# A column roll of an 8192 x 8192 matrix: all long row pieces issued on SP's ring, where SP and ACT had alternate rows

## The chip, the cores and the metric

The kernel runs on one core of one Trainium2 chip. The metric is the device time of one execution in microseconds (us), lower is better. Times before are given as the median of four runs; the profile is of one further execution. A core has 16 DMA engines; transfers reach them through rings (queues): one hardware ring for the transfers that SP issues, one for those of ACT, and a software ring for those of POOL.

## The reference

```python
def setup_inputs():
    return {
        "x": np.random.randn(8192, 8192).astype(np.float32),
        "shift": 100,
    }

def reference(x, shift):
    return np.roll(x, shift, axis=1)
```

Each row is rotated right by 100 columns: output columns 100 to 8191 are input columns 0 to 8091, and output columns 0 to 99 are the input's last 100. It is data movement alone: 268.4 MB in, 268.4 MB out.

## The kernel before

With `shift` 100, `s` is 100, and `a`, the column that divides the two ways of moving data, is 256 (100 rounded up to 128, plus 128, since it is at most 384). `g` is 156.

**Long row pieces** (line 43). Output columns 256 to 8191 are copied from HBM to HBM, without going through on-chip memory. Rows are taken in 128 blocks of 64 (`blocks`, loop variable `c`). In a block, the 64 rows are seen as 16 groups (`e`) of 4 consecutive rows (`j`). One DMA moves row `j` of all 16 groups: 16 rows of 7,936 floats (31,744 B each), 496 KB, one row for each DMA engine. The list `engines` (line 25) gives rows `j` = 0 and 2 to SP (`nc.sync`) and `j` = 1 and 3 to ACT (`nc.scalar`). In the last four blocks each DMA is cut in two column halves at `mid` (column 4224), 248 KB each. That makes 124 x 4 = 496 whole and 4 x 4 x 2 = 32 half DMAs: 248 whole and 16 half on each of the two engines.

**Heads** (lines 68 to 82). Output columns 0 to 255 go through on-chip memory on POOL's software ring. For each of 4 groups of 2,048 rows, POOL loads three tiles `t` of leading pieces (line 73) and two parts of `h` (lines 74 and 77), DVE copies pieces from `t` into `h` (lines 75 and 78), and after all loads POOL writes each `h` with four DMAs (line 82), 16 in all. That is 36 DMAs.

**What sets the order.** Each engine issues its DMAs in the order of the program. The tile framework gives every DMA from SP or ACT one of eight semaphores, DMAHW0 to DMAHW7, in turn, and a DMA waits until the earlier one with its semaphore has landed. As the two engines alternate, SP's DMAs have the semaphores 1, 3, 5, 7 and ACT's 0, 2, 4, 6: the first four on each engine wait for no transfer, and each later one waits for the one four places before it on its own engine, which is eight places before it in the program. There is no other wait between pieces, since they touch disjoint parts of the output. POOL's DMAs have semaphores of their own and wait for earlier loads, for DVE's copies and for their own earlier writes.

On a DMA engine, a row shows in the trace as one packet of 31,744 B (15,872 B for a half), followed on its ring by a packet of 4 B, which counts up the DMA's semaphore. Head packets have up to 4,400 B.

Of the kernel before, what the change touches and what calls it, by code (L numbers as in the profile page):

```python
# [1 line left out]

# [4 lines left out]


@with_exitstack
def kernel(  # L10
    ctx: ExitStack,
    tc: tile.TileContext,
    x: bass.AP,
    shift: int,
    out: bass.AP,
):
    nc = tc.nc
    n_rows, n_cols = x.shape
    s = shift % n_cols
    a = -(-s // 128) * 128  # L20
    if 0 < a <= 384 and a + 128 <= n_cols:
        a += 128
    g = a - s
    P = nc.NUM_PARTITIONS
    engines = [nc.sync, nc.scalar]
    n_chunks = 16
    rows = n_rows // n_chunks

    xm = x.rearrange("(c e j) w -> c j e w", e=16, j=4)
    om = out.rearrange("(c e j) w -> c j e w", e=16, j=4)
    if a < n_cols:
        blocks = n_rows // 64
        mid = (a + n_cols) // 256 * 128
        for c in range(blocks):
            parts = ((a, mid), (mid, n_cols)) if c >= blocks - 4 and a < mid else ((a, n_cols),)  # L40
            for j in range(4):
                for lo, hi in parts:
                    engines[j % 2].dma_start(out=om[c, j, :, lo:hi], in_=xm[c, j, :, lo - s:hi - s])
    if a == 0:
        return


    if a > 512:
        for i in range(n_chunks):
            r = slice(i * rows, (i + 1) * rows)  # L50
            nc.gpsimd.dma_start(out=out[r, :s], in_=x[r, n_cols - s:])
            if g > 0:
                nc.gpsimd.dma_start(out=out[r, s:a], in_=x[r, :g])
        return

    Q, J = 4, 4  # L60
    n_st = n_rows // (P * Q * J)
    reads = ctx.enter_context(tc.tile_pool(name="reads", bufs=n_st))
    heads = ctx.enter_context(tc.tile_pool(name="heads", bufs=n_st))
    xt = x.rearrange("(k p j q) c -> k q p j c", q=Q, j=J, p=P)
    ot = out.rearrange("(k p j q) c -> k q p j c", q=Q, j=J, p=P)
    tiles = []
    for k in range(n_st):
        t = reads.tile([P, Q - 1, J, a], x.dtype)
        h = heads.tile([P, Q, J, a], x.dtype)
        for q in range(1, Q):  # L70
            lead = bass.AP(tensor=x.tensor, offset=(k * P * J * Q + q) * n_cols - s,
                           ap=[[J * Q * n_cols, P], [Q * n_cols, J], [1, a]])
            nc.gpsimd.dma_start(out=t[:, q - 1], in_=lead)  # L73
        nc.gpsimd.dma_start(out=h[:, Q - 1, :, :s], in_=xt[k, Q - 1, :, :, n_cols - s:])  # L74
        nc.vector.tensor_copy(h[:, :Q - 1, :, :s], t[:, :, :, :s])  # L75
        if g > 0:
            nc.gpsimd.dma_start(out=h[:, 0, :, s:], in_=xt[k, 0, :, :, :g])  # L77
            nc.vector.tensor_copy(h[:, 1:, :, s:], t[:, :, :, s:])  # L78
        tiles.append(h)
    for k, h in enumerate(tiles):  # L80
        for q in range(Q):
            nc.gpsimd.dma_start(out=ot[k, q, :, :, :a], in_=h[:, q])  # L82


# [1 line left out]
_INS = ['x', 'shift']  # L86
_OUTS = [((8192, 8192), 'float32')]

_NUMBERS = {'shift': 100}


# [26 lines left out]
```

## Time and profile before

| what | value |
|---|---|
| median of 4 runs | 817.65 us (816.1 to 818.37) |
| the profiled execution's own time | 817.73 us |
| its span, first to last instruction | 815.6 us |
| DVE busy | 7.7 us, 8 instructions |
| POOL busy | 28.8 us, 40 instructions |
| bytes moved by the DMA engines | 276.89 MB, 340 GB/s over the span |
| DMA packets | 21,573, of them 9,025 under 512 B |

The span is read from the first to the last instruction of the core; the execution's own time has some 2 us more around it. Busy times of engines leave out the instructions that issue DMAs on SP and ACT. "Share" beside a DMA queue is the time its packets took, as a share of the span of 16 DMA engines; the share of a stretch is the mean busy share of these engines. GB/s counts each byte moved once, also where it is read from HBM and written to HBM. The time of a DMA "to landing" runs from its issue to the last count on its semaphore. The queues q1 and q10 are the two hardware rings of SP and ACT, and q0 is POOL's software ring.

### The profile page before, as it was taken

What the parts mean: (1) busy time and instruction counts of PE and PEld (TensorE: products, weight loads), DVE (VectorE), ACT (ScalarE), POOL (GpSimd) and SP (SyncE); (2) the same over time, 40 slices, a digit from 0 to 9 for tenths busy, and PEclk for the clock granted to TensorE, in tenths of its full rate; (3) what the DMA queues carried; (4) which work ended last, traced back from release to release, by engine and by line L of the source; (5) the groups of instructions that cost most, each with busy time, mean ns of one, the idle gap of its engine ahead of it and who ended that gap; (6) DMA issues with size and microseconds to landing.
All of it is one profiled execution on the core that took longest, in us unless ns stands there. A gap on an engine that the chain in (4) does not pass through costs nothing. (4 is left out here: it accounts for less than half of the span.)

```text
span 815.6 us, 633 instructions
## 1 busy us (share of the span) xinstructions
DVE 7.7 (1%) x8; POOL 28.8 (4%) x40
## 2 busy tenths in 40 slices
DVE  0000000000000000000000000000000000000000
POOL 3000000000010000000000000000000000000000
DMA  9999999999999999999999999999999999999998
GB/s 312 345 344 343 347 349 344 358 355 352 348 349 365 351 359 352 358 353 358 337 332 333 330 335 339 330 335 336 332 332 332 334 326 349 325 335 333 330 309 297
DMA packets 21573, 276.89 MB, mean 340 GB/s; under 512 B 9025, under 2 KB 9025, under 8 KB 13121
## 3 DMA queue, kind: packets, MB, share of 16 engines
q1 hardware_dynamic: 8448, 130.04, 46.5%
q10 hardware_dynamic: 8448, 130.04, 45.5%
q0 software_dynamic: 4672, 16.78, 7.0%
q14 instruction: 5, 0.03, 0.0%
HBM read 268.44 MB, written 268.44 MB: 658 GB/s over the span
## 5 line engine op out<-in xcount | busy, mean ns | idle before, releaser
L82 POOL DMA_DIRECT2D out_dram<-h x16 | 13.2, 825 | 196.2 <-DMA out_dram<-h 109.8
L73 POOL DMA_DIRECT2D t<-in_x_dram x12 | 9.5, 793 | 60.3 <-DMA h<-in_x_dram 30.2
L75 DVE COPY h<-t 128x1200 f32<-128x1200 f32 x4 | 3.1, 784 | 232.3 <-DMA t<-in_x_dram 232.3
L78 DVE COPY h<-t 128x1872 f32<-128x1872 f32 x4 | 4.9, 1224 | 0.0
L74 POOL DMA_DIRECT2D h<-in_x_dram x4 | 3.0, 747 | 45.7 <-DMA t<-in_x_dram 45.7
L77 POOL DMA_DIRECT2D h<-in_x_dram x4 | 3.0, 749 | 41.5 <-DMA t<-in_x_dram 41.5
L99 POOL MEMSET const-float32-0.0<- 128x1 f32 x1 | 0.1, 98 | 0.2 <-issue 0.2
L99 POOL MEMSET const-bfloat16-1.0<- 128x1 bf16 x1 | 0.1, 102 | 0.0
L99 POOL MEMSET const-float32-1.0<- 128x1 f32 x1 | 0.1, 99 | 0.0
L99 POOL MEMSET const-uint8-127<- 128x1 uint8 x1 | 0.1, 99 | 0.0
## 6 DMA issues: line engine op xcount, KB each, us to landing
out_dram<-in_x_dram SPq DMA_DIRECT2D x248, 496.0 KB, 12.6
out_dram<-in_x_dram ACTq DMA_DIRECT2D x248, 496.0 KB, 12.6
out_dram<-h POOLq DMA_DIRECT2D x16, 512.0 KB, 113.2
t<-in_x_dram POOLq DMA_DIRECT2D x12, 512.0 KB, 95.1
out_dram<-in_x_dram SPq DMA_DIRECT2D x16, 248.0 KB, 6.0
out_dram<-in_x_dram ACTq DMA_DIRECT2D x16, 248.0 KB, 6.1
h<-in_x_dram POOLq DMA_DIRECT2D x4, 312.0 KB, 93.4
h<-in_x_dram POOLq DMA_DIRECT2D x4, 200.0 KB, 97.4
```

What stands on the lines that cost most here:

```text
L73: nc.gpsimd.dma_start(out=t[:, q - 1], in_=lead)
L74: nc.gpsimd.dma_start(out=h[:, Q - 1, :, :s], in_=xt[k, Q - 1, :, :, n_cols - s:])
L75: nc.vector.tensor_copy(h[:, :Q - 1, :, :s], t[:, :, :, :s])
L77: nc.gpsimd.dma_start(out=h[:, 0, :, s:], in_=xt[k, 0, :, :, :g])
L78: nc.vector.tensor_copy(h[:, 1:, :, s:], t[:, :, :, s:])
L82: nc.gpsimd.dma_start(out=ot[k, q, :, :, :a], in_=h[:, q])
L99: nc = _bacc.Bacc("TRN2", target_bir_lowering=False, num_devices=1)
```

## The change

The list of two engines goes, and line 43 (42 in the changed kernel) issues every long piece from SP. Pieces, their sizes and their order stay; the heads stay on POOL.

```diff
-    engines = [nc.sync, nc.scalar]
     n_chunks = 16
     rows = n_rows // n_chunks
...
             for j in range(4):
                 for lo, hi in parts:
-                    engines[j % 2].dma_start(out=om[c, j, :, lo:hi], in_=xm[c, j, :, lo - s:hi - s])
+                    nc.sync.dma_start(out=om[c, j, :, lo:hi], in_=xm[c, j, :, lo - s:hi - s])
```

In the built program ACT has no DMA any more, and SP has 496 whole and 32 half ones in the order in which both engines had them. The eight semaphores go round over SP's DMAs alone: its first eight wait for no transfer, and each later one waits for the one eight places before it. POOL's and DVE's instructions are the same.

## The prediction

> **What bounds the kernel now.** I first read the table of stretches (columns: window, its length, busy us and instructions of DVE and of POOL, TensorE clock, mean busy share of the 16 DMA engines, GB/s moved) and the DMA queue rows of the page.
>
> ```profile
> 0.00:20.00 20.00, 0.00 (x0) 6.31 (x12) 1.00 0.91 310
> 20.00:200.00 180.00, 5.87 (x6) 12.37 (x15) 1.00 1.00 349
> 200.00:380.00 180.00, 1.83 (x2) 10.17 (x13) 1.00 1.00 354
> 420.00:600.00 180.00, 0.00 (x0) 0.00 (x0) 1.00 1.00 334
> 600.00:780.00 180.00, 0.00 (x0) 0.00 (x0) 1.00 0.99 333
> 780.00:800.00 20.00, 0.00 (x0) 0.00 (x0) 1.00 0.88 296
> 800.00:816.00 16.00, 0.00 (x0) 0.00 (x0) 1.00 0.79 291
> ```
>
> ```profile
> q1 hardware_dynamic: 8448, 130.04, 46.5%
> q10 hardware_dynamic: 8448, 130.04, 45.5%
> q0 software_dynamic: 4672, 16.78, 7.0%
> ...
> HBM read 268.44 MB, written 268.44 MB: 658 GB/s over the span
> ```
>
> The DMA engines are busy from start to end; no compute engine matters. The GB/s column seems to say that three rings (349, 354) are faster than two (334, 333). It counts each byte once, though, while a row piece touches HBM twice (read and write) and a head byte once (its other side is on chip). In 20 to 200 us the queue rows of that window give 55.34 MB of pieces and 7.45 MB of heads: (2 x 55.34 + 7.45) / 180 us = 656 GB/s at HBM. In 200 to 380 us: (2 x 55.85 + 7.79) / 180 = 664. In 420 to 780 us, with two rings: (2 x 119.79 + 0.28) / 360 = 666. So HBM traffic is level while the number of working rings falls from three to two.
>
> The packet records tell the same. I put them in order engine by engine (the trace names no engine, but a record begins within 4 ns of the end of the one before it on its engine, so nearly all chain up). A whole row, 31,744 B, takes 1.173 us at its fastest, 27.1 GB/s per engine or 433 GB/s for 16. Its mean is 1.37, 1.43 and 1.51 us in the three stretches: where head packets (159 ns each) take engine time, rows get shorter. Engines thus wait in their rows for something that they share, about 0.34 us of 1.51, and HBM is what fits.
>
> Next, the waits of the SP queue and the landing times of the issues:
>
> ```profile
> SPq L43 <- DMA out_dram<-in_x_dram: 670.1, 260, 4.0
> ```
>
> ```profile
> out_dram<-in_x_dram SPq DMA_DIRECT2D x248, 496.0 KB, 12.6
> out_dram<-in_x_dram ACTq DMA_DIRECT2D x248, 496.0 KB, 12.6
> out_dram<-h POOLq DMA_DIRECT2D x16, 512.0 KB, 113.2
> ```
>
> Of 264 issues on SP, 260 wait: each DMA has one of eight semaphores and waits for the DMA eight places before it. The program order has semaphores 1, 3, 5, 7 on SP and 0, 2, 4, 6 on ACT, so four DMAs are in flight on each. 12.6 us is about eight times the 1.55 us that one row DMA costs the machine (815.6 / 528).
>
> **The change, part by part.** Bytes, pieces, their order and the 36 POOL DMAs are unchanged. In the new program order SP has all 528 DMAs, with semaphores 0 to 7 in turn: each still waits for the one eight before. The total in flight stays eight, on one ring.
>
> Removed: 264 ACT issues of 516 ns (136 us), all beside transfers and off the path. Added on SP: 264 x 510 ns = 135 us. At the start SP's issues are 0.63 us apart (1.33, 1.98, 2.61 us from the first event), so SP needs 528 x 0.63 = 333 us of a span of 816; the cover is the eight DMAs in flight. Value: nothing. Without the cover a piece would wait 0.63 us for its issue; the bound would be 333 us, still far below.
>
> Start: a first issue lands rows on all 16 engines, each row needs at least 1.17 us, and the next issue comes 0.63 us later; one ring fills the engines. Nothing.
>
> Last four blocks: 32 half pieces of 248 KB, one per 0.72 us now (14 pairs of issues in 20.3 us). SP at 0.63 has little room, and a delay of one issue (0.5 us) is no longer covered by six microseconds of queue so well: up to +2 us. Against it, a piece's semaphore packet now follows its own data; today the order on an engine is mostly row of one ring, row of the other, then both semaphore packets, so that the first waits for a neighbour's row. Slots come free earlier: down to -2 us. I take 0, since the two act on the same wait.
>
> Heads: engines take turns between rings. Today a software packet comes once in about every row; with one hardware ring it gets a turn after the row and one after its semaphore packet, up to two per row. The heads can finish near 200 instead of 385 us, but nobody waits for them, and the HBM bytes are the same: nothing, if HBM sets the pace.
>
> The one price that the trace does not show in bulk is the order **row, semaphore, row, semaphore** on one ring. In the records there are 83 places where an engine did row, semaphore, row of one ring with nothing between: the gap ahead of the second row has a median of 4 ns, and a quarter of these rows take 1.175 us, the minimum. So there is no fixed bubble. But where an engine alternates row and semaphore for three rows or more (307 runs, any ring), it spends 1.540 us per row, 1.4% over the others at that moment; where it does two rows and then two semaphores (1,567 runs), 1.509, 1.4% under. Upper bound: 528 x 0.031 = 16 us, if nothing absorbs it. Lower bound: 0, or below by what earlier release gives (6 us, see the third case). An engine's cost is taken out of its 0.34 us of waiting for HBM, and stretches with 2 to 3% idle engines move no less at HBM (600 to 620 us: share 0.986, 671 GB/s). So I take 0 and keep both ends.
>
> The Trainium skill, "DMA: Bandwidth & Descriptors", section "Queues, rings and completion order", speaks against the change: a semaphore increment is a strongly ordered write, landing only after every earlier write of that engine. The same page, "Latency and other measured facts", gives HBM access as 0.2 us on average and 2 us under high load. If a ring stood still for 0.2 us per row, an estimate by that page, 528 of them would add 106 us; the 4 ns gaps above do not show that, though they are few.
>
> Sum: the profiled execution was 817.73 us (span 815.6 and 2.1 around it); 817.7 + 0 + 0 + 0 = **817.7 us**, against a median of 817.65.
>
> **The rivals.**
> - **Slower: the semaphore packet after every row costs engine time that HBM does not absorb.** For it: the 1.540 against 1.509 us. Against it: the level HBM rate and the 4 ns gaps. It applies all through, and decides once the cost exceeds what the engines now wait for HBM. Full price 817.7 + 16 = 834; with half absorbed, 826. I give 826.
> - **One ring holds fewer than eight DMAs.** The trace shows four on a ring, never more. With half the bytes in flight, the nearest row is the half-piece stretch at 296 GB/s against 333: 817.7 x 333 / 296 = 920. It is the case where the change does not do what the semaphores say.
> - **Faster: earlier release and shorter stalls.** Share 0.88 and 0.79 in the last 36 us is 20 x 0.12 + 16 x 0.21 = 5.8 us idle, of which 1.6 us lie after the last data; 0.5% idle in 420 to 780 us is 1.8 us. If all goes: 817.7 - 4.2 - 1.8 = 811.7. Half of it and a little from HBM, which no row prices: 812. That HBM itself moves more with rows going strictly in turn cannot be excluded: its 20 us stretches in 420 to 780 us lie between 648 and 683 GB/s, so 1% or so (8 us) below 812, 804, is the far end.
>
> **How the numbers follow.** A measurement of this kernel can tell about 0.2% (1.6 us) from no change. HBM cap, no change: 0.38. Slower at 826: 0.34. One ring too short: 0.02. Faster at 812: 0.26. A part of the first case falls just outside 1.6 us on either side, and a part of the outer ones inside, so faster is 0.28, same 0.34, slower 0.38. The range 804 to 834 us takes in both bounds of the semaphore cost and the faster case; outside it remain the short ring and larger movements of HBM. The forecast's own range is 816 to 819.5.
>
> **What would show it.** Right: SP's waits fall from 670 to about 500 us (816 less 333), landing stays near 12.5 us, one hardware queue at some 92% of the engines, HBM near 658 GB/s, heads done near 200 us. The slower case: the mean of a whole row still near 1.5 us or above after the heads, with the mean rate after 420 us under 330 GB/s and landing above 12.6. Short ring: SP's waits gone into long issues and engine share near 0.9. Faster: the last two rows of the table of stretches above 300 GB/s and the share there above 0.9. The forecast is wrong if the HBM rate with only one ring at work leaves 655 to 675 GB/s.

## The result and the profile after

The changed kernel takes 818.38 us (median of 52 runs, 816.18 to 822.52), the kernel before 816.93 us (median of 76 runs). The ratio is 1.0020, 95% interval 1.0014 to 1.0026: 1.6 us slower by the ratio, 1.5 us by the medians, just at the border of what the prediction called no change. The profiled execution took 819.14 us, with a span of 817.0. In the experiments, which all ran on one chip, the kernel before takes 830 us, so each of them is given with its ratio to the kernel before as it ran beside it.

The stretches, with the columns of the table before (window, length, busy us of DVE and of POOL, clock, share of the DMA engines, GB/s):

```profile
0.00:20.00 20.00, 0.00 (x0) 7.04 (x13) 1.00 0.91 321
20.00:200.00 180.00, 7.70 (x8) 21.80 (x27) 1.00 1.01 362
200.00:380.00 180.00, 0.00 (x0) 0.00 (x0) 1.00 1.00 341
420.00:600.00 180.00, 0.00 (x0) 0.00 (x0) 1.00 1.00 332
600.00:780.00 180.00, 0.00 (x0) 0.00 (x0) 1.00 1.00 332
780.00:800.00 20.00, 0.00 (x0) 0.00 (x0) 1.00 0.94 314
800.00:817.00 17.00, 0.00 (x0) 0.00 (x0) 1.00 0.86 300
```

The DMA engines are as full as before. POOL's work, which reached past 370 us, is now done in the second row: in 20 to 200 us GB/s rises from 349 to 362, since more of the bytes are head bytes that touch HBM once. At HBM nothing rose. The queue rows of that stretch (packets, MB, share) are

```profile
q1 hardware_dynamic: 3324, 52.77, 78.1%
q0 software_dynamic: 3467, 12.40, 22.8%
```

which makes (2 x 52.77 + 12.40) / 180 us = 655 GB/s, against 656 before. From the page, the queues over the whole span, and HBM:

```profile
q1 hardware_dynamic: 16896, 260.08, 92.7%
q0 software_dynamic: 4672, 16.78, 6.7%
...
HBM read 268.44 MB, written 268.44 MB: 657 GB/s over the span
```

One ring carries what two carried, 92.7% against 46.5 + 45.5%, and HBM moves 657 GB/s against 658. SP's waits and the issues, with KB each and us to landing:

```profile
SPq L42 <- DMA out_dram<-in_x_dram: 529.0, 499, 2.0
```

```profile
out_dram<-in_x_dram SPq DMA_DIRECT2D x496, 496.0 KB, 12.4
out_dram<-h POOLq DMA_DIRECT2D x16, 512.0 KB, 59.2
out_dram<-in_x_dram SPq DMA_DIRECT2D x32, 248.0 KB, 5.5
```

SP issues twice as often and still waits 529 us for landings; a whole DMA lands in 12.4 us, so eight are in flight. POOL's writes land in 59 us where they took 113: the software ring gets its turns more often. In 20 to 200 us it moved 12.40 MB, before 7.45. The last head DMA has landed at 262 us, before at 485.

Where do the 1.6 us lie? I summed the packet records' HBM bytes over time in both profiles. The two stay within about 1 us of each other until half of the bytes are through (270 of 537 MB: 412.8 and 413.8 us), then the changed kernel falls behind slowly, by 2.4 us at 510 MB, and ends 1.5 us behind. In the stretch without heads it moves 663 GB/s at HBM, before 667. In this pair of profiles it is a small loss along the second half, with no single wait in it. One pair of profiles cannot place so small a loss; a second pair, under the last experiment, does not repeat it there.

### The profile page after: what moved, and what is told of

Its sections match the earlier page's. It is cut to its first block, busy times and chain, and to the rows that moved or that the text cites. A ratio compares the mean times of both kernels' runs of the same rounds, so it can differ in the third digit from the quotient of the medians.

```text
span 817.0 us, 633 instructions
## 1 busy us (share of the span) xinstructions
DVE 7.7 (1%) x8; POOL 28.8 (4%) x40
## 2 busy tenths in 40 slices
DMA packets 21572, 276.89 MB, mean 339 GB/s; under 512 B 9024, under 2 KB 9024, under 8 KB 13120
## 3 DMA queue, kind: packets, MB, share of 16 engines
q1 hardware_dynamic: 16896, 260.08, 92.7%
## 6 DMA issues: line engine op xcount, KB each, us to landing
out_dram<-in_x_dram SPq DMA_DIRECT2D x496, 496.0 KB, 12.4
```

## The experiments

Four theories of the small loss were put to the test. Theory A: the semaphore packet right after each row costs the single ring some HBM rate. Theory B: the heads, which now finish early, cause it. Theory C: SP's issues limit. Theory E, formed after the first runs: one ring moves a little less in the long stretch and wins some back in the half pieces. The experiments ran in three sets, each with the kernel before beside it.

**Without heads, two rings and one.** The function returns after the long pieces:

```diff
-    if a == 0:
+    if a < n_cols:
         return
```

> This kernel leaves the heads out (output columns 0 to 255 are not written) and has the long pieces on SP and ACT as before. It is the partner of the next one. Both theories: 520.1 MB of HBM traffic at the 0.6665 MB per us that the kernel before showed between its last head packet and its first half piece is 780.4 us; with 2.7 us before the first data, about 0.7 us lost in the half pieces and 2.1 us around the span, about 786 us.

> Heads left out (output columns 0 to 255 are not written), all long pieces on SP. Theory A (a semaphore packet right after every row makes the single ring move less at HBM, 0.6635 against 0.6665 MB per us in the stretch without heads): the loss is there without heads too and longer, 520.1/0.6635 = 783.9 us, so about 3 us slower than the partner with two rings, less 1 us gained in the half pieces: +2 to +3 us. Theory B (the loss comes from the heads, which are done by 261 instead of 485 us and leave a longer stretch without them, or from their double turns): no heads, no loss: within 1 us of the partner, or faster by the 1 us gained at the end.

Measured: 800.06 us with two rings (ratio 0.9643, 0.9625 to 0.9661) and 800.32 us with one (0.9641, 0.9622 to 0.9659). With heads the kernel before took 830.5 us in this set. The 786 us expected for two rings was for a kernel before of 817 us; 0.9643 of that is 788. No loss of one ring can be seen here, which speaks against theory A and for B, as far as intervals of 0.2% on either side reach: the 2 to 3 us that A expected lie at their edge. The pair says something about the bound too. The pages' HBM rows:

```profile
HBM read 260.05 MB, written 260.05 MB: 652 GB/s over the span
```

(the same for both kernels). Without heads the bytes that DMA engines move fall by 6.1% (276.89 to 260.05 MB), those at HBM by 3.1%; the time falls by 3.6%. That is much nearer to the fall at HBM than to that at the engines; 0.5% is left over.

**Two rows per engine in a DMA.**

```diff
+    xi = x.rearrange("(c e j) w -> c e j w", e=16, j=4)
+    xo = out.rearrange("(c e j) w -> c e j w", e=16, j=4)
...
+            if c < blocks - 4:
+                for j in range(0, 4, 2):
+                    nc.sync.dma_start(out=xo[c, :, j:j + 2, a:n_cols], in_=xi[c, :, j:j + 2, a - s:n_cols - s])
+                continue
```

With two rings, `engines[j // 2]` stands in place of `nc.sync`.

> As before, but each whole DMA takes two consecutive rows per DMA engine (32 rows, 992 KB; rows 0 and 1 on SP, 2 and 3 on ACT), the last four blocks as they were. Half as many semaphore packets and twice the bytes in flight. Theory A: a semaphore packet costs engine time, which two rings already halve by taking them in pairs; at most 1 to 2 us faster than before. Theory B: no change within 1 us.

> Two rows per engine and DMA as in the kernel above, all on SP. The order on an engine is row, row, semaphore packet. Theory A: as many semaphore stops as in the two-ring kernel before, so the loss of one ring is gone or halved: 0 to 1 us against the two-ring partner, 1 to 2 us faster than the changed kernel. Theory B: the heads get their turns at a different rhythm still, the loss of 1.5 to 2 us against the two-ring partner stays.

Measured: 842.07 us (1.0134, 1.0110 to 1.0158) and 844.15 us (1.0168, 1.0147 to 1.0188): both slower than before by far more than any theory had. Half the semaphore packets did not help, which speaks against A, though a larger loss from something else lies over it; the 2.1 us between the partners fit B, but the intervals overlap. About half of the loss is at the end: the last tenth of the HBM bytes takes the one-ring kernel 90.0 us, and the changed kernel 83.4 on the same chip. Two rows of the stretches, first of the two-ring kernel, then of the one-ring kernel:

```profile
780.00:800.00 20.00, 0.00 (x0) 0.00 (x0) 1.00 0.99 321
800.00:840.00 40.00, 0.00 (x0) 0.00 (x0) 1.00 0.70 241
```

```profile
780.00:800.00 20.00, 0.00 (x0) 0.00 (x0) 1.00 0.98 314
800.00:842.00 42.00, 0.00 (x0) 0.00 (x0) 1.00 0.76 260
```

For the last 40 us the engines are idle for a quarter to a third of the time, against 0.88 and 0.79 busy in the kernel before. Each DMA's semaphore counts 16 engines, so the trace shows how far apart they end one and the same DMA. From 100 to 770 us that is 17.6 and 18.3 us here, and 6.3 us in the kernel before. With DMAs twice as long, and so twice the bytes in flight, the engines drift apart nearly three times as far. That the early ones have nothing left at the end fits the idle engines; it is not shown by itself, and length and bytes in flight were changed together.

**Only reading.** Each long row is read into on-chip memory and not written; no heads:

```diff
+            for j in range(4):
+                t = land.tile([P, (n_cols - a) // 8], x.dtype)
+                nc.sync.dma_start(out=t, in_=xm[c, j, :, a - s:n_cols - s].rearrange("e (k w) -> e k w", k=8))
+    if a < n_cols:
+        return
```

(`land` has 16 buffers; the two-ring kernel has `engines[j % 2]`.)

> Leaves out the heads and every write of the output: the long pieces are only read, each row into eight partitions of on-chip memory (eight packets of 3,968 B per row and engine, then the semaphore packet), on SP and ACT in turn. HBM traffic is halved. If HBM sets the pace of the kernel before, the engines now run at their own speed: head packets of 4,096 B took 159 ns, so 8 x 154 ns x 512 rows = 631 us. If a row's 1.51 us is the engine's or the ring's own time, 512 x 1.51 = 773 us.

> The same (no heads, no write of the output), all on SP. With no wait for HBM to absorb it, the cost of a semaphore packet after every row shows: by the theory that it costs up to 31 ns, up to 16 us over the partner with two rings; by the theory that it costs nothing, within 2 us of it. SP needs 512 x 0.63 = 323 us for its issues and is not the bound in either.

Measured: 1,057 us with two rings, its runs spread from 1,010 to 1,076, and 1,083 us with one (1,074 to 1,102; ratio 1.301, 1.295 to 1.307). Neither expectation holds: reading alone is slower than copying. The pages' HBM rows, two rings and then one:

```profile
HBM read 260.05 MB, written 0.00 MB: 250 GB/s over the span
```

```profile
HBM read 260.05 MB, written 0.00 MB: 240 GB/s over the span
```

The packets of 3,968 B take 259 and 270 ns where the fastest take 153, at 0.37 to 0.38 of the HBM traffic of the copy (240 and 250 against 652 GB/s). Something in this way of reading binds, and I did not find what. The pair was to price the semaphore packet at the engines' own speed; it does not, and given the spread of the two-ring runs even the 25 us between them are no price.

**Halves everywhere.**

```diff
-            parts = ((a, mid), (mid, n_cols)) if c >= blocks - 4 and a < mid else ((a, n_cols),)
+            parts = ((a, mid), (mid, n_cols)) if a < mid else ((a, n_cols),)
```

> All pieces cut in halves of 248 KB, on SP and ACT in turn: twice the DMAs and semaphore packets, half the bytes in flight. If half the bytes in flight are too few, the kernel goes at the rate of its half-piece stretch, 296 GB/s against 333 before: about 9 to 12% slower. If HBM sets the pace as long as the engines are busy for 0.9 of the time (329 GB/s between 800 us and the last data in the kernel before): within 2%, and the end is better since the engines cannot drift so far apart.

> Halves everywhere, all on SP: 1,024 issues at 0.63 us are 645 us of some 820, one piece per 0.77 us. Theory A (semaphore packets cost HBM rate on one ring): twice as many of them, so twice the loss against the two-ring partner, 3 to 5 us. Theory C (SP's issues become the limit when 248 KB pieces go through it alone): over 10 us slower than the partner, with SP waiting for landings under 100 us. Theory B (heads): 1 to 2 us, as in the changed kernel.

Measured: 832.3 us with two rings (1.0033, 1.0014 to 1.0053) and 831.54 us with one (1.0021, 1.0001 to 1.0041); before 830.41. Twice the semaphore packets and half the bytes in flight cost 0.2 to 0.3%, and on one ring no more than on two. That is the end of theory A, and of C: SP still waits for landings for 237 us with 1,024 issues.

```profile
SPq L42 <- DMA out_dram<-in_x_dram: 237.5, 604, 1.2
```

The "1 to 2 us" put down for theory B did not come either: there are heads here, yet one ring is not slower. This does not refute B, in which it is early heads that cost time: here they end early on both, at 183 us on two rings and 144 us on one. The stretches are alike (two rings, then one):

```profile
200.00:780.00 580.00, 0.00 (x0) 0.00 (x0) 1.00 1.00 326
...
800.00:832.00 32.00, 0.00 (x0) 0.00 (x0) 1.00 0.94 309
```

```profile
200.00:780.00 580.00, 0.00 (x0) 0.00 (x0) 1.00 1.00 326
...
800.00:831.00 31.00, 0.00 (x0) 0.00 (x0) 1.00 0.92 300
```

The engines end a DMA 2.0 us apart in both. The half pieces at the end of the kernel before, at 296 GB/s, were thus no measure of a smaller window: 248 KB pieces by themselves run at 326 GB/s here.

**The changed kernel again, and all on ACT.** The second has `nc.scalar` in place of `nc.sync` on line 42.

> The changed kernel itself, on one chip with the next three. Against the kernel before it was 1.0014 to 1.0026 over many runs. If that belongs to the kernel, about +1.6 us here too; if it depends on the chip, anything from -1 to +3 us, as the pairs of the earlier runs (-0.8 with halves, +0.3 without heads, +2.1 with two rows) would allow.

> All long pieces on ACT's ring in place of SP's. If what counts is one ring in place of two, the same as the changed kernel within 1 us. If it is SP (its issue, 510 ns, or its other duties), different by more: ACT's issue is 516 ns, 6 ns longer, which lies beside the transfers.

Measured: 831.5 us (1.0016, 1.0002 to 1.0031) and 831.54 us (1.0020, 1.0008 to 1.0033), before 830.01. The loss is there in the experiments too, and it is the same on ACT: it belongs to one ring in place of two, not to SP.

**No half pieces at the end.**

```diff
-            parts = ((a, mid), (mid, n_cols)) if c >= blocks - 4 and a < mid else ((a, n_cols),)
+            parts = ((a, mid), (mid, n_cols)) if c >= blocks and a < mid else ((a, n_cols),)
```

> Two rings, no half pieces at the end: all 512 DMAs are whole. The engines end further apart: with 12 us in flight in place of 6, 2 to 5 us slower than before.

> One ring, no half pieces at the end. Theory E (one ring moves 0.1 to 0.4% less at HBM in the long stretch, 1 to 2.5 us, and wins back 1 us in the half pieces): the win goes, so 2 to 3 us slower than the two-ring partner, more than the changed kernel is slower than before. If the difference comes from the half pieces alone (SP issues each 0.63 us while one is due every 0.72): no difference from the partner.

Measured: 831.5 us with two rings (1.0022, 1.0010 to 1.0034) and 835.12 us with one (1.0064, 1.0046 to 1.0082). The two-ring kernel loses 1.5 us, less than the 2 to 5 expected. Without the halves one ring is 3.6 us slower than two, with them 1.5 us. This is somewhat more than the 2 to 3 us of theory E, and only in part at its place. In the two profiled executions (831.47 and 836.0 us) the last data land 4.8 us apart. Of these, 2.8 us arise ahead of the last 17 MB at HBM, where E had 1 to 2.5 us; 2.0 us arise in them (27.6 us on two rings, 29.6 us on one), where E had nothing. With half pieces the last 17 MB take no longer on one ring than on two (26.4 and 26.6 us in the profiles of the result). The last stretch of the two-ring and of the one-ring kernel:

```profile
785.00:810.00 25.00, 0.00 (x0) 0.00 (x0) 1.00 0.99 333
810.00:830.00 20.00, 0.00 (x0) 0.00 (x0) 1.00 0.72 243
```

```profile
785.00:810.00 25.00, 0.00 (x0) 0.00 (x0) 1.00 1.01 333
810.00:835.00 25.00, 0.00 (x0) 0.00 (x0) 1.00 0.68 226
```

Until 810 us both go at 333 GB/s; then the one-ring kernel has 5.7 MB left (226 GB/s x 25 us) where the other has 4.9 (243 x 20), and its engines are idle for 0.32 of the time, against 0.28.

Up to its last four blocks the two-ring kernel here is the kernel before. So its profile can be held against the changed kernel's on the same chip. The stretch from 540 to 780 us with two rings, then of the changed kernel, then with one ring and no halves:

```profile
540.00:780.00 240.00, 0.00 (x0) 0.00 (x0) 1.00 1.00 327
```

```profile
540.00:780.00 240.00, 0.00 (x0) 0.00 (x0) 1.00 1.00 328
```

```profile
540.00:780.00 240.00, 0.00 (x0) 0.00 (x0) 1.00 1.00 325
```

The changed kernel moves no less here than two rings do. It is 1.5 us behind when 100 MB have passed at HBM and 1.1 us at 510 MB. The 663 against 667 GB/s of the first pair is thus not repeated, and where in the kernel the loss arises is not shown.

The drift of the engines sorts these runs. Drift is the time between the first and the last engine's end of one DMA, as a mean over those that begin to land from 100 to 770 us. The table gives it with each pair's times, and the time at which the last head DMA has landed:

| pieces | two rings: drift, heads done, time | one ring: drift, heads done, time | one ring slower by |
|---|---|---|---|
| as before (drift and heads from the profiles of the result, times of the last set) | 6.3 us, 485, 830.0 | 7.2 us, 262, 831.5 | 1.5 us |
| no halves at the end | 6.4 us, 493, 831.5 | 7.4 us, 264, 835.1 | 3.6 us |
| two rows in a DMA | 17.6 us, 654, 842.1 | 18.3 us, 350, 844.2 | 2.1 us |
| halves everywhere | 2.0 us, 183, 832.3 | 2.0 us, 144, 831.5 | -0.8 us |
| no heads | 6.1 us, none, 800.1 | 7.1 us, none, 800.3 | 0.3 us |

On one ring the engines drift about 1 us further with whole rows, and where the pieces are half as long they do not. Where one ring lost time, it drifted further. The pair without heads drifts as far apart and loses nothing measurable, so the drift alone is not shown to be the cause. The heads sort the pairs at least as well. Where one ring lost 1.5 to 3.6 us, its heads were done 223 to 304 us earlier than on two rings; with halves everywhere they were done only 39 us earlier, and without heads there was no loss. That is theory B. No kernel with whole rows kept the heads late on one ring or made them early on two, so B stands open as a rival to the drift.

## Why the prediction was right

The forecast was no change at 817.7 us; the runs gave 818.38. That the two times lie 0.7 us apart is in part luck: the 817.7 started from a profiled run of 817.73, and over 76 runs the kernel before has 816.93. The change itself was put at 0 and is 1.5 to 1.6 us. This lies on the border between the forecast's case of no change (0.34) and its slower case (0.38), and does not decide between them; against the 826 us given for the slower case, it is far nearer to no change.

- **HBM sets the pace: right as far as it was tested.** HBM moves 655 GB/s with heads and 663 to 667 without, on one ring as on two; time goes nearly with HBM bytes when the heads go. In the slower experiments a whole row still takes 1.173 us at its fastest, while its mean rises to 1.53 to 1.55 us (without heads): the engines can go as fast there, and what they wait for is slower. That this is HBM, and not something else that all engines share, is argued; the read-only kernels were to test it directly and did not. Two readings were looser than they look. The 159 ns of a head packet is its median; the mean is 213. And the rate of a single 20 us stretch depends on how the rows at its borders are counted: with each row's bytes spread over its time, 600 to 620 us has 662 GB/s and not 671, and the stretches from 420 to 780 us lie between 651 and 674. The argument from idle engines holds all the same, since the two stretches with shares of 0.98 and 0.97 (620 to 660 us) have 667 and 664.
- **SP's extra issues cost nothing: right.** SP's waits were to fall to about 500 us and are 529. Even 1,024 issues leave 237 us of waiting.
- **Eight in flight on one ring: right.** 12.4 us to landing; the rival of a ring too short, 920 us, is out. Its price was wrong too: half the bytes in flight cost 0.3%, not 12%. The 296 GB/s it came from was a draining end and no rate of a small window.
- **Row, semaphore, row: 0 taken, 16 us as the bound.** Zero was the better value. In the changed kernel some 5,000 rows follow their own ring's semaphore packet directly, with a median gap within 4 ns and a fastest row of 1.17 us. The 83 places of the forecast were fewer still if each record is paired with the nearest end (5 whole rows), so they showed little. The 1.4% that such runs lagged in the kernel before was no price of the semaphore packet: doubling these packets cost one ring nothing that can be measured (ratio 1.0021 against 1.0016). That estimate compared engines that happened to be in one order or the other, and the order may as well have followed from a slow engine as caused it.
- **The end, 0 taken out of -2 to +2 us: right by accident of the halves.** The share in the last rows rose (0.88 to 0.94, 0.79 to 0.86), the first of them past the 0.9 that the faster rival named, but the last 17 MB took 26.4 us after and 26.6 before. More engines were busy for the same bytes in the same time. Without halves the end of one ring costs 2 us, so it is the halves that made 0 come true.
- **Heads: date wrong, cost small.** POOL's last issue is at 198 us, but the last head DMA has landed at 262. The forecast forgot the 59 us to landing; by the same measure the heads of before ended at 485 us, not 385. That early heads cost nothing holds to 0.2%; whether they cost that 0.2% is open.
- **The slower rival's signs.** The mean of a whole row stays near 1.5 us after the heads (1.52 in 420 to 780 us, 1.51 before), as it said; the rate there is 332 GB/s, not under 330, and landing 12.4 us, not above 12.6.
- **What was missed** is the 0.2%: a small disadvantage of one ring for whole rows. It is one ring's (ACT gives the same), and it is not the semaphore packets', nor SP's. It goes with a wider drift of the engines and with an earlier end of the heads; which of the two costs the time, or whether it is something else, stays open.

## What to carry to other kernels

Here all DMA engines were busy and the bytes at HBM per microsecond stayed level while the number of rings changed, and rings and issuing engines were worth tenths of a per cent. To see this, count HBM bytes in each stretch, not the GB/s of the table, which counts a byte once whether it touches HBM once or twice. What a smaller piece or window costs is not to be read from the end of a kernel, where the engines run out of work. Longer DMAs with more bytes in flight were not free here: the engines drifted further apart, and about half of the loss lay at the end. A difference of 0.2% is not to be placed from one pair of profiles.

## What the runs showed of the hardware that was not expected

- Two rows per engine and DMA, 992 KB, made the kernel 1.3% slower (ratio 1.0134, 1.0110 to 1.0158) and let the engines end one DMA 18 us apart; 248 KB pieces kept them 2 us apart at a cost of 0.3%.
- Reading rows from HBM into eight partitions of 3,968 B each went at 240 to 250 GB/s, less than the copy from HBM to HBM reads (some 326 GB/s beside as much written, on the same chip).
- A software ring beside one hardware ring gets through its work in about half the time that it takes beside two: its 36 DMAs were done at 262 us in place of 485, its writes landed in 59 us in place of 113, and in 20 to 200 us its packets took 22.8% of the engines' time in place of 16.6%.
- The same kernel before took 817 us in the runs of the result and 830 us in the experiments, a difference eight times that of the change.
